# A 2,080-byte pitch for the tiles that TensorE streams in a two-layer hybrid encoder trunk

## Chip, cores and metric

The kernel runs on 1 core of one Trainium2 chip. The metric is the device time of one execution in microseconds. The kernel before takes 2495.84 us (median of 3 runs, 2495.49 to 2499.09).

## What is computed

Two layers over x, 512 tokens of 1,024 channels in float32. Cut to what matters here:

```python
for l in range(DEPTH):
    x = x + 0.5 * swiglu(rms_norm(x, norm_ffn1[l]), ffn1_wi[l], ffn1_wo[l])   # 1024 -> 2 x 2816 -> 1024
    p = rms_norm(x, norm_mix[l]) @ w_in[l]
    x = x + concat(rwkv7(p_a), chunk_attention(p_q, p_k, p_v), pool(p_c)) @ w_out[l]
    x = x + memory_cross_attention(rms_norm(x, norm_cross[l]), rms_norm(mem, norm_mem[l]), ...)
    x = x + 0.5 * swiglu(rms_norm(x, norm_ffn2[l]), ffn2_wi[l], ffn2_wo[l])
```

The four SwiGLU half steps hold most of the arithmetic; then come the input and output projections of the mixers and the four projections of the cross attention.

## The kernel before, in words

Channels lie on the 128 partitions and tokens in the free dimension, so x is eight tiles of 128x512 float32, 2,048 bytes in each partition. Every dense product is made in three passes over exact parts: an operand is split into a high part (a rounded copy by ScalarE, `act` at L75) and a low part (the rest, by VectorE, L69 or L72), and `mm3` issues high x high, high x low and low x high into one PSUM bank (all matmuls of helpers have line L78).

The parts live in three pools. **wp** holds two raw weight tiles of 4,096 bytes (L115, filled by SP's DMA at L116), and three buffers each of `whi` and `wlo` (L149 and L150), 2,048 bytes. A weight tile of 1,024 columns becomes two pairs of `whi` and `wlo`; each holds four slices of 128 columns, 512 bytes apart, that TensorE loads as stationary operand. **hp** holds the eight x tiles and sixteen slots of `hslot` (L83): the normed activations `hhi` and `hlo` for the eight channel blocks k, later the mixers' outputs (`mahi`, `mbhi`, `mchi` and their low parts) and half of the cross attention's (`xohi`, `xolo`). **hid** is opened by each SwiGLU half step and holds 44 tiles `fhi` and `flo` for the 22 blocks of gated values (L282 and L283).

In `ffn`, for each of 22 blocks f, `proj` streams the sixteen h tiles past the weights of the gate (`pg`) and of the up product (`pu`): 8 blocks k times 3 passes, each with its own weight slice. Then ScalarE and VectorE make the gated values and split them. Eight products `po` follow, each streaming the 44 tiles of hid past 22 slices. The mixers (`pin`, `pbvf`, `pout`) stream tiles of hp in the same way, beside the recurrence and the attention, in an order that rates written into the kernel set. In `proj_tok_steps` (`pqk`, `pxq`) the roles are exchanged: 128 tokens of an h tile are stationary and 256 columns of `whi` or `wlo` stream. The cross attention has its own pool with further streamed tiles (`xphi`, `xo`) that the change doesn't touch.

Where a tile lies in its partition follows from the pools, which stand one behind the other in the order in which they are opened: const, wp, hp, tp, bp, and then hid or the pool of a mixer or of the cross attention. In wp and hp all tiles are multiples of 2,048 bytes, so every `whi`, `wlo` and h tile begins at the same place within 2,048 bytes (96 bytes past a multiple). Between hp and hid the one tile that isn't a multiple of 2,048 bytes is `rtok`, 16 bytes that take 32; so the tiles of hid begin 32 bytes further within 2,048 (128 bytes past a multiple).

Of the kernel before, what the change touches and what calls it, by code (L numbers as in the profile page):

```python
# [9 lines left out]
F32R = mybir.dt.float32r  # L10
# [4 lines left out]
P = 128  # L15
T = 512
# [15 lines left out]
LEAD, DENSE_RATE, ATT_RATE = 15, (1.0, 0.61, 0.98), 0.65  # L32
TURN_RATE = (0.5, 0.9)

PAR = {}
# [18 lines left out]
def trunk(tc, I, out, depth=DEPTH):  # L54
    nc = tc.nc
    ctx = ExitStack()
    with ctx:
        const = ctx.enter_context(tc.tile_pool(name="const", bufs=1))
        wp = ctx.enter_context(tc.tile_pool(name="wp", bufs=1))
        hp = ctx.enter_context(tc.tile_pool(name="hp", bufs=1))  # L60
# [21 lines left out]

        def hslot(name, dt=F32R, shape=None):  # L83
            return hp.tile(shape or [P, T], dt, tag="h", name=name, bufs=16)

# [24 lines left out]
        x = [xslot("x") for _ in range(KD)]  # L110
# [20 lines left out]
        ones = const.tile([P, P], F32, name="ones")  # L131
# [6 lines left out]

# [1 line left out]
        def split(o_hi, o_lo, src):  # L140
# [3 lines left out]
        def weights(ap, n):  # L144
            raw = ahead.pop(0) if ahead else load_raw(ap, n)
            r = []
            for c in range(0, n, 512):
                e = min(512, n - c)
                hi = wp.tile([P, 512], F32R, tag="whi", name="whi", bufs=3)  # L149
                lo = wp.tile([P, 512], F32R, tag="wlo", name="wlo", bufs=3)  # L150
                split(hi[:, :e], lo[:, :e], raw[:, c:c + e])
                r.append((hi, lo))
            return r
# [20 lines left out]
        def proj_tok_steps(banks, ap, acts):  # L174
            """banks[i][128 tokens, 2, 256] = act[tokens]^T W, for W = ap [128, 8, 256]."""
            w = []
            for k0 in (0, 4):
                w += weights(ap[:, k0:k0 + 4].rearrange("p k m -> p (k m)"), 1024)
                for k in range(k0, k0 + 4):
                    s = slice(k % 2 * 256, k % 2 * 256 + 256)  # L180
                    wh, wl = w[k // 2]
                    ah, al = acts[k]
                    for b, p in enumerate(banks):
                        for i in range(2):
                            c = slice((2 * b + i) * P, (2 * b + i + 1) * P)
                            st = k == 0 and i == 0
                            mm(p[:, i], ah[:, c], wh[:, s], st, False)
                            mm(p[:, i], al[:, c], wh[:, s], False, False)
                            mm(p[:, i], ah[:, c], wl[:, s], False, k == 7 and i == 1)
                    yield  # L190
# [8 lines left out]

# [1 line left out]
        ssq = {}  # L201
# [13 lines left out]
        def update(k, p, scale=None, spill=False, fetch=None):  # L215
            """x += scale * p; x leaves for DRAM or is fetched from there around the mixers."""
            if fetch is not None:
                x[k] = fetch
                nc.sync.dma_start(out=x[k], in_=x_dram[k])
            if scale is None:  # L220
                tt(x[k], x[k], p, add)
            else:
                stt(x[k], p, scale, x[k], mult, add)
            if spill:
                nc.sync.dma_start(out=x_dram[k], in_=x[k])
            square_in(k)

        def tok_rstd(sq, n, o, scale, e, tag="sm"):
            """o[128 tokens, n / 128] = 1/sqrt(scale * sum over channels of sq + e)."""
            p = bank(tag, "ptok")  # L230
            for i in range(n // P):
                mm(p[:, i:i + 1], sq[:, i * P:(i + 1) * P], ones[:, 0:1])
            act(o, p[:, :n // P], AF.Sqrt, bias=e, scale=scale)
            nc.vector.reciprocal(out=o, in_=o)

        def rstd(bcast=True, tag="sm"):
            """1/rms of x for each token, with the tokens on the rows and, on request, on the columns."""
            rt = tp.tile([P, 4], F32, tag="rtok", name="rtok", bufs=1)
            tok_rstd(ssq["a"], T, rt, 1.0, eps, tag)
            r = None  # L240
            if bcast:
                p = bank(tag, "psn")
                for i in range(4):
                    mm(p[:, i * P:(i + 1) * P], rt[:, i:i + 1].to_broadcast([P, P]), ident)
                r = tp.tile([P, T], F32, tag="rstd", name="rstd", bufs=1)
                act(r, p, AF.Copy)
            return r, rt
# [11 lines left out]

# [1 line left out]
        def ffn(l, which):  # L261
            h = norm(l, f"norm_{which}")
            wi, wo = I[f"{which}_wi"][l], I[f"{which}_wo"][l]
            hid = []
            with tc.tile_pool(name="hid", bufs=1) as hidp:
                for f in range(KF):
# [14 lines left out]
                    tt(u, u, z, mult)  # L281
                    hi = hidp.tile([P, T], F32R, name=f"fhi{f}")  # L282
                    lo = hidp.tile([P, T], F32R, name=f"flo{f}")  # L283
                    split(hi, lo, u)
                    hid.append((hi, lo))
                for m in range(KD):
                    p = bank(ROT[(m + 4) % 8], "po")
# [4 lines left out]

# [1 line left out]
        def mixer(l):  # L294
# [4 lines left out]
            with mx as mp:  # L299
# [29 lines left out]

                # values  # L330
                v = [shifted(6 + j, f"v{j}") for j in range(3)]
# [27 lines left out]

                # the low-rank inputs  # L360
                t9 = shifted(9, "t9")
# [4 lines left out]

                # while x is in DRAM its eight slots hold scratch of the preparation and then q and k of the attention
                # (later its output) and the biases
                xs = [xslot(f"xs{i}") for i in range(8)]
# [63 lines left out]

                # RWKV-7 by chunks of 64, two at a time
                halves = (slice(0, 64), slice(64, 128))
# [19 lines left out]
                def systems(q, o):  # L455
                    """For the pairs 2q and 2q + 1 of chunks, in two sets of heads g, g + 2, g + 4: the masked
                    scores and the inverse of each chunk's triangular system."""
                    nn = mp.tile([P, 2, 3, 2, HD], F32, tag="nn", name="nn", bufs=1)
                    ata, at = [], []
                    for c4 in range(4):  # L460
# [13 lines left out]
                        yield  # L474
                    # doubling the blocks of b: sources in the even blocks, targets in the odd ones. F holds no more
                    # than its blocks, so that the products need a mask only for which blocks pair up; and until
                    # the last step its 32-blocks hold all of it
                    F = []
# [32 lines left out]
                def keyrows(p):  # L511
                    """Keys on the rows, decayed to the chunk's end."""
                    tr = [None, None]
# [16 lines left out]
                def chain(p):  # L530
                    """The state through chunks 2p and 2p + 1, and what they put out."""
                    ata, at, F, tr = sys[p]["ata"], sys[p]["at"], sys[p]["F"], trs[p]
                    y = mp.tile([P, 6, HD], F32, tag="y", name="y", bufs=2)
                    for c2 in range(2):
# [40 lines left out]
                        yield  # L575
                    # group norm, bonus, gate
                    gs = mp.tile([P, 6], F32, tag="gs", name="gs", bufs=2)
# [77 lines left out]

                # attention over all earlier chunks and the own one
                def attend(j, bq, bk, bvt):
# [38 lines left out]
                def pool():  # L696
                    # trailing windows: sums by doubling
                    pwt = mp.tile([P, 2, P], F32, tag="pwt", name="pwt")
                    nc.sync.dma_start(out=pwt, in_=I["poolw"][l])
                    for j in range(2):  # L700
                        def trail(o, i, n):
                            """o = i + i from n tokens before."""
                            nc.gpsimd.tensor_copy(out=o[:, :n], in_=i[:, :n])
                            tt(o[:, n:], i[:, n:], i[:, :T - n], add)
# [55 lines left out]

                # the recurrence sets the pace; the dense products and the attention take steps at these rates beside it
                live = {"r": recurrence(), "d": dense(), "a": attention()}
# [29 lines left out]

# [1 line left out]
        def cross(l):  # L794
            with tc.tile_pool(name=f"cx{l}", bufs=1) as cp:
# [26 lines left out]
                def head(w, acts, n, r, gain, tag, o, b):  # L822
                    """An RMS-normed head; the step it leaves behind puts the channels on the partitions, as high and low parts."""
                    nt = n // P
# [156 lines left out]

# [1 line left out]
def _pack(w, n=P):  # L983
    """[K, M] -> [M / n, 128, K / 128, n]: one contiguous run a partition for each tile of M."""
    K, M = w.shape
    return np.ascontiguousarray(w.reshape(K // P, P, M // n, n).transpose(2, 1, 0, 3))
# [85 lines left out]
```

## Time and profile before

| | |
|---|---|
| median of 3 runs | 2495.84 us (2495.49 to 2499.09) |
| profiled execution, first to last instruction | 2493.6 us; its time as a whole isn't listed |
| TensorE matmul | busy 2460.9 us (99%), 14,058 instructions |
| TensorE weight load | busy 2001.1 us (80%) |
| VectorE, ScalarE, GpSimd | busy 52%, 40%, 7% |
| granted TensorE clock | 1.000 over the span |

Busy matmul time joins intervals that overlap: a matmul's duration is taken from its first column to its end, and the next one starts before that. What a matmul costs TensorE is the distance from its start to the next start, which is shorter than the duration that a row gives; where two groups of matmuls are alike but for their operands and neither waits, their durations differ by what their distances differ. Window counts include an instruction that is cut by the window's edge.

### The profile page before, as it was taken

What the parts mean: (1) busy time and instruction counts of PE and PEld (TensorE: products, weight loads), DVE (VectorE), ACT (ScalarE), POOL (GpSimd) and SP (SyncE); (2) the same over time, 40 slices, a digit from 0 to 9 for tenths busy, and PEclk for the clock granted to TensorE, in tenths of its full rate; (3) what the DMA queues carried; (4) which work ended last, traced back from release to release, by engine and by line L of the source; (5) the groups of instructions that cost most, each with busy time, mean ns of one, the idle gap of its engine ahead of it and who ended that gap; (6) DMA issues with size and microseconds to landing.
All of it is one profiled execution on the core that took longest, in us unless ns stands there. A gap on an engine that the chain in (4) does not pass through costs nothing.

```text
span 2493.6 us, 35631 instructions
## 1 busy us (share of the span) xinstructions
PE 2460.9 (99%) x14058; PEld 2001.1 (80%) x14058; DVE 1300.3 (52%) x2361; ACT 1007.5 (40%) x1804; POOL 184.9 (7%) x246
## 2 busy tenths in 40 slices
PE   8999999999999999999999999999999999999999
PEld 6888887877689888888888888867776898888887
DVE  5444335757575644443344443367676756444422
ACT  4333334434465543333333333343344655433322
POOL 1000002101020000000000000021111201000000
PEclk9999999999999999999999999999999999999999
DMA  3223333210242222323332233322102422222332
GB/s 134 95 99 94 106 114 102 69 45 20 68 143 99 71 93 94 102 93 93 93 99 96 95 98 110 119 72 68 45 25 70 148 88 71 94 100 94 99 110 87
DMA packets 72504, 225.27 MB, mean 90 GB/s; under 512 B 8177, under 2 KB 13201, under 8 KB 72337
## 3 DMA queue, kind: packets, MB, share of 16 engines
q1 hardware_dynamic: 72336, 223.00, 27.5%
q8 instruction: 110, 1.80, 0.3%
q14 instruction: 58, 0.47, 0.1%
HBM read 215.89 MB, written 7.08 MB: 89 GB/s over the span
## 4 chain that ended last, share of the span: by engine, by line
PE 95%; DVE 2%; issue 1%; ACT 1%; DMA 1%; POOL 0%; POOLq 0%; ACTq 0%; DVEq 0%; SPq 0%
PE po L78 20%; PE pu L78 20%; PE pg L78 19%; PE pxq L78 5%; PE pin L78 4%; PE pxw L78 3%; PE pqk L78 3%; PE pout L78 3%; PE pxv L78 2%; PE pbs L78 1%; PE pbvf L78 1%; PE pf L78 1%; PE ptt L78 1%; PE pbo L78 1%; PE pr L78 1%; PE psc L78 1%
## 5 line engine op out<-in xcount | busy, mean ns | idle before, releaser
L75 ACT ACTIVATE whi<-raw 128x512 fp32r<-128x512 f32 (+1 forms) x806 | 493.8, 614 | 964.9 <-PE po L78 323.9
L69 DVE TENSOR_TENSOR wlo<-raw,whi 128x512 fp32r<-128x512 f32 (+1 forms) x806 | 550.5, 685 | 570.4 <-ACT whi L75 566.7
L78 PE MATMUL pg<-hhi,whi 128*128 128x512 f32 x704 | 275.4, 391 | 6.6 <-ACT whi L75 6.6
L78 PE MATMUL po<-fhi,whi 128*128 128x512 f32 x704 | 278.1, 395 | 0.0
L78 PE MATMUL po<-fhi,wlo 128*128 128x512 f32 x704 | 278.1, 395 | 0.0
L78 PE MATMUL po<-flo,whi 128*128 128x512 f32 x704 | 278.1, 395 | 0.0
L78 PE MATMUL pg<-hlo,whi 128*128 128x512 f32 x704 | 275.4, 391 | 2.6 <-DVE hlo L72 2.6
L78 PE MATMUL pu<-hhi,wlo 128*128 128x512 f32 x704 | 274.0, 389 | 0.7 <-DVE wlo L69 0.7
L78 PE MATMUL pg<-hhi,wlo 128*128 128x512 f32 x704 | 274.5, 390 | 0.0
L78 PE MATMUL pu<-hhi,whi 128*128 128x512 f32 x704 | 273.9, 389 | 0.0
L78 PE MATMUL pu<-hlo,whi 128*128 128x512 f32 x704 | 273.9, 389 | 0.0
L69 POOL TENSOR_TENSOR ssa<-ssa,sq 128x512 f32<-128x512 f32 x63 | 86.7, 1377 | 1238.4 <-ACT sq L75 1237.8
L78 PEld LDWEIGHTS pg<-hhi,whi 128*128 128x128 f32 x704 | 132.6, 188 | 34.1 <-ACT whi L75 6.6
L78 PEld LDWEIGHTS po<-flo,whi 128*128 128x128 f32 x704 | 131.9, 187 | 32.4
L78 PEld LDWEIGHTS po<-fhi,whi 128*128 128x128 f32 x704 | 131.9, 187 | 32.4
L78 PEld LDWEIGHTS po<-fhi,wlo 128*128 128x128 f32 x704 | 131.9, 187 | 32.2
L78 PEld LDWEIGHTS pg<-hlo,whi 128*128 128x128 f32 x704 | 132.3, 188 | 31.7 <-DVE hlo L72 4.9
L78 PEld LDWEIGHTS pu<-hhi,wlo 128*128 128x128 f32 x704 | 132.1, 188 | 28.4 <-DVE wlo L69 1.2
L78 PEld LDWEIGHTS pg<-hhi,wlo 128*128 128x128 f32 x704 | 132.6, 188 | 27.6 <-DVE wlo L69 0.3
L78 PEld LDWEIGHTS pu<-hhi,whi 128*128 128x128 f32 x704 | 132.1, 188 | 27.7
L78 PEld LDWEIGHTS pu<-hlo,whi 128*128 128x128 f32 x704 | 132.3, 188 | 27.4
L69 DVE TENSOR_TENSOR z<-pg,rstd 128x512 f32<-128x512 f32 x88 | 60.9, 692 | 134.0 <-PE pg L78 124.4
(305 smaller groups left out, 4010.7 us busy)
## 6 DMA issues: line engine op xcount, KB each, us to landing
raw<-in_ffn_wi_dram SPq DMA_DIRECT2D x175, 512.0 KB, 3.5
raw<-in_ffn_wo_dram SPq DMA_DIRECT2D x64, 512.0 KB, 3.5
raw<-in_w_in_dram SPq DMA_DIRECT2D x30, 512.0 KB, 3.5
raw<-in_ffn_wo_dram SPq DMA_DIRECT2D x32, 384.0 KB, 3.1
raw<-in_x_wk_dram SPq DMA_DIRECT2D x16, 512.0 KB, 3.6
raw<-in_x_wv_dram SPq DMA_DIRECT2D x16, 512.0 KB, 3.5
raw<-in_x_wq_dram SPq DMA_DIRECT2D x16, 512.0 KB, 3.5
raw<-in_w_qk_dram SPq DMA_DIRECT2D x12, 512.0 KB, 3.6
```

The lines of the kernel that those rows point to most:

```text
L69: (eng or nc.vector).tensor_tensor(out=o, in0=a, in1=b, op=op)
L75: nc.scalar.activation(out=o, in_=i, func=f, **k)
L78: nc.tensor.matmul(o, lhsT=w, rhs=x, start=start, stop=stop)
```

## The change

Tiles of `hslot`, of `whi` and `wlo` and of `fhi` and `flo` get rows of 520 elements, of which the first 512 are used. Nothing else in the program is different: the same instructions in the same order with the same shapes. Behind the first longer tile everything in the partition moves up: x by 192 bytes, the pools behind hp by 704 bytes. Comments and docstrings are blanked in the new file (not shown), as are two arguments of `hslot` that no call used.

```diff
+ROW = T + 8
...
-        def hslot(name, dt=F32R, shape=None):
-            return hp.tile(shape or [P, T], dt, tag="h", name=name, bufs=16)
+        def hslot(name, dt=F32R):
+            return hp.tile([P, ROW], dt, tag="h", name=name, bufs=16)[:, :T]
...
-                hi = wp.tile([P, 512], F32R, tag="whi", name="whi", bufs=3)
-                lo = wp.tile([P, 512], F32R, tag="wlo", name="wlo", bufs=3)
+                hi = wp.tile([P, ROW], F32R, tag="whi", name="whi", bufs=3)[:, :T]
+                lo = wp.tile([P, ROW], F32R, tag="wlo", name="wlo", bufs=3)[:, :T]
...
-                    hi = hidp.tile([P, T], F32R, name=f"fhi{f}")
-                    lo = hidp.tile([P, T], F32R, name=f"flo{f}")
+                    hi = hidp.tile([P, ROW], F32R, name=f"fhi{f}")[:, :T]
+                    lo = hidp.tile([P, ROW], F32R, name=f"flo{f}")[:, :T]
```

## Rows read from the trace of the kernel before

**Rows 1.** The page: the span, busy time of each engine, and the chain by engine

```profile
span 2493.6 us, 35631 instructions
...
PE 2460.9 (99%) x14058; PEld 2001.1 (80%) x14058; DVE 1300.3 (52%) x2361; ACT 1007.5 (40%) x1804; POOL 184.9 (7%) x246
...
PE 95%; DVE 2%; issue 1%; ACT 1%; DMA 1%; POOL 0%; POOLq 0%; ACTq 0%; DVEq 0%; SPq 0%
```

**Rows 2.** Stretches: gate and up products, then second products; columns in the first line

```profile
core 0: us, PE busy (x) PEld busy (x) DVE busy (x) ACT busy (x) POOL busy (x), PEclk, DMA share, GB/s
1000.00:1100.00 100.00, 100.00 (x443) 82.84 (x442) 47.05 (x73) 34.74 (x55) 0.00 (x0) 1.00 0.29 95
1140.00:1240.00 100.00, 100.00 (x430) 80.34 (x429) 37.04 (x53) 31.52 (x53) 7.76 (x6) 1.00 0.32 96
```

**Rows 3.** Groups of matmuls by shape: busy us, mean ns | idle before, releaser

```profile
L78 PE MATMUL po<-fhi,whi 128*128 128x512 f32 x704 | 278.1, 395 | 0.0
...
L78 PE MATMUL pg<-hhi,whi 128*128 128x512 f32 x704 | 275.4, 391 | 6.6 <-ACT whi L75 6.6
L78 PE MATMUL pg<-hlo,whi 128*128 128x512 f32 x704 | 275.4, 391 | 2.6 <-DVE hlo L72 2.6
L78 PE MATMUL pg<-hhi,wlo 128*128 128x512 f32 x704 | 274.5, 390 | 0.0
L78 PE MATMUL pu<-hhi,wlo 128*128 128x512 f32 x704 | 274.0, 389 | 0.7 <-DVE wlo L69 0.7
```

**Rows 4.** Timeline of TensorE in the up product and in the second product: start us, duration

```profile
1089.66 0.39 PE L78 MATMUL pu<-hhi,wlo 128*128 128x512 f32 x1
...
1090.34 0.39 PE L78 MATMUL pu<-hhi,wlo 128*128 128x512 f32 x1
...
1189.71 0.40 PE L78 MATMUL po<-fhi,whi 128*128 128x512 f32 x1
...
1190.41 0.39 PE L78 MATMUL po<-fhi,whi 128*128 128x512 f32 x1
```

**Rows 5.** Groups of matmuls by shape: value and output product of the cross attention

```profile
L78 PE MATMUL pxv<-whi,mlo 128*128 128x512 f32 x64 | 25.3, 395 | 0.0
L78 PE MATMUL pxv<-wlo,mhi 128*128 128x512 f32 x64 | 25.3, 395 | 0.0
L78 PE MATMUL pxw<-xohi,whi 128*128 128x512 f32 x64 | 25.3, 395 | 0.0
L78 PE MATMUL pxw<-xolo,whi 128*128 128x512 f32 x64 | 25.2, 393 | 0.0
L78 PE MATMUL pxw<-xohi,wlo 128*128 128x512 f32 x64 | 24.9, 389 | 0.0
```

**Rows 6.** Matmuls of tile pxw, 874 to 880 us: duration ns min/median/max, first and last start

```profile
L78 PE MATMUL pxw<-xo,whi x8: 392/396/402, 876.4 to 878.7; 128*128 128x512 f32 x8
L78 PE MATMUL pxw<-xohi,whi x6: 389/394/397, 873.6 to 879.9; 128*128 128x512 f32 x6
L78 PE MATMUL pxw<-xolo,whi x5: 389/397/398, 873.9 to 879.4; 128*128 128x512 f32 x5
L78 PE MATMUL pxw<-xohi,wlo x5: 387/389/389, 874.1 to 879.7; 128*128 128x512 f32 x5
L78 PE MATMUL pxw<-xo,wlo x4: 396/398/399, 876.9 to 879.0; 128*128 128x512 f32 x4
```

**Rows 7.** Timeline of TensorE in an input projection of the mixer

```profile
390.55 0.39 PE L78 MATMUL pin<-hhi,wlo 128*128 128x512 f32 x1
...
393.95 0.39 PE L78 MATMUL pin<-hhi,wlo 128*128 128x512 f32 x1
```

**Rows 8.** Groups of matmuls by shape: 256 columns of weights stream past tokens

```profile
L78 PE MATMUL pxq<-wlo,hhi 128*128 128x256 f32 x256 | 72.8, 284 | 0.0
...
L78 PE MATMUL pxq<-wlo,mhi 128*128 128x256 f32 x128 | 36.2, 283 | 0.4 <-DVE wlo L69 0.4
```

## The prediction

> **What bounds the kernel now.** I read the page's totals and its chain first: TensorE is busy for 99% of the span and 95% of the chain that ended last is its matmuls; VectorE and ScalarE stand at 52% and 40% [rows 1]. So a time can only come from how fast matmuls follow one another. The windows show that in two stretches of 100 us in which TensorE never pauses and the granted clock is 1.00 (2.4 GHz): 443 matmuls of the gate and up products, but only 430 of the second products, of the same shape [rows 2]. That is 225.7 and 232.6 ns for one (edges counted alike). The timeline gives the same: three up matmuls take 0.68 us, three second products 0.70 us [rows 4]. And the groups by shape: 389 ns duration in pu, 390 and 391 in pg, 395 in po (one of three equal groups of pu and of po stands there), with next to no idle time in front [rows 3]; the difference of 6 ns is the difference in distance again. So **matmuls of one shape, without a wait, differ by 6 ns by which tiles they read.**
>
> What differs is where the tiles lie. In pg and pu the streamed h tile and the weight tile begin at the same place within 2,048 bytes, and the four weight slices at steps of 512; so streamed tile and weight slice agree within 512 bytes always. In po they are 32 bytes apart. Two more groups are apart, and both are slow: the value product of the cross attention streams whi past mlo, 32 bytes apart the other way, 395 ns [rows 5]; and xo, 352 bytes apart, has medians of 396 and 398 ns [rows 6]. The same rows hold the control: xohi and xolo, tiles of hp that agree with the same weights, come right behind xo in the same product and range from 387 to 398, median 389 to 397. So agreement doesn't help at once; after a change of relation some matmuls pass before they run at 389. In the mixer, left alone, h tiles run at that rate too: fifteen starts from 390.55 to 393.95 us, 0.227 us each [rows 7].
>
> **The change part by part.**
>
> *Where tiles lie after it.* Each weight tile is 32 bytes further than the one before (six of them), each h slot too (sixteen), and hp begins 6 x 32 = 192 bytes later. H slot i and weight buffer j are then 192 + 32 x (i - j) bytes apart, taken within 512: they agree for one slot in sixteen. For hid it is 736 + 32 x (i - j): again one in sixteen. The relation also changes with every block k and between high and low part, so nothing stays agreed for long enough to settle.
>
> *Gate and up products.* 4,224 matmuls lose the agreement, except one in sixteen. The price is bounded by 392 (the mean of 395, 393 and 389 over the three groups of xohi and xolo) and 395 (po, pxv) [rows 3, 5]. I take 395, since the relation is wrong nearly always as in po, and not half of the time as in xohi. pu: 2,112 x (395 - 389) = 12.7 us. pg: 2,112 x (395 - 390.7) = 9.1 us. Less a sixteenth: 20.4 us. By the low bound it is 2,112 x 3 + 2,112 x 1.3 = 9 us.
>
> *Mixer projections and output.* pin, pbvf and pout stream h tiles 1,104 times (576, 144 and 384). Their group means hold waits, so what share runs at 389 I can't read from them; from a stretch like rows 7 I take about two thirds: 1,104 x 6 x 2/3 = 4.4 us, between 0 and 6.6.
>
> *Second products.* 2,112 matmuls at 395 are apart now and will be, by other distances. One in sixteen agrees: -0.8 us. Bounds: all of them fall to 389, -12.7 us; or they rise to xo's 397, +4 us.
>
> *Streams of 256 columns* (pqk, pxq). Weights stream past h tiles. With agreement the low weights take 284 ns, and 283 past the memory's tiles, which are 32 bytes off [rows 8]. The 1,344 of them that stream past h tiles change by 1 ns at most: 0, between -1.3 and +1.3 us.
>
> *Everything else.* ScalarE and VectorE write and read the same elements; were they slower by a little, their idle half hides it [rows 1, 2]. SP issues the same DMAs to the raw tiles, whose pitch stays. 704 bytes more are used in a partition, and no buffer is lost. I cost these at nothing.
>
> *Sum.* 20.4 + 4.4 - 0.8 = 24 us. The profiled execution's span of 2,493.6 us, with 2.2 us around it if it was a median run, stands for the median of 2,495.84; so 2,495.8 + 24 = **2,520 us**. With the low price for gate and up and nothing for the mixer it is 2,505; with 395 throughout, and xo's price for po, 2,495.8 + 21.8 + 6.6 + 4 + 1.3 = 2,530. A little above that, 2,536, if a new relation is worse than the three that rows show.
>
> **The rivals.**
>
> *Equal places are the clash (faster).* The agreement in pg and pu could be merely a milder form of a clash that all streams have because each begins where the one before it began. 256 columns more cost 389 - 284 = 105 ns [rows 3, 8], so 512 columns stream in 210 ns; the distance is 227, and up to 17 ns of each matmul are not streaming. If staggering returns half, 8 ns on 7,632 matmuls of 512 columns (4,224 + 2,112 + 1,104 + 192 of xohi and xolo), the time is 2,435; a quarter, 2,465. It decides once pg and pu fall below 389. For it: the 17 ns are real, and thirteen of the sixteen distances stand in no row. Against it: in rows 6 the place of the streamed tile changes twice in six microseconds and no matmul falls under 387. The Trainium skill's TensorE: Matmul & The Clock Gate (Back-to-back issue gap) gives 512 / 2.4 + 2.5 = 216 ns for a single isolated matmul's gap; by that figure a stream rid of all clashes would bring an estimated 11 ns and 2,412 us. No row here shows 216. Chance 0.20.
>
> *Only the second products gain.* They reach 389 and the first ones hold it, because a coarser property of the place counts: 2,495.8 - 12.7 = 2,483. Against it: pxv streams whi from the very place of the h tiles and is slow. Chance 0.06.
>
> *It doesn't matter (same).* Either the 6 ns come from something else than the place, or the relation repeats every 64 bytes: then two of three weight buffers still agree, a third of the first products loses (7.3 + 1.5 us) and two thirds of the second gain (-8.5 us): 2,496 either way. Against the latter: softer evidence, only that xphi and the values, 128 bytes apart, aren't shown to settle. By the Trainium skill's SBUF — State Buffer (Who interferes with whom) TensorE has two independent read ports, one for the streamed operand and one for weights, and never waits on anyone; by that rule the place of a tile is free and the time stays at 2,496. Rows 3 speak against the rule, with 389 against 395 at equal shape and no wait. Chance 0.12.
>
> *The forecast.* Slower, 2,505 to 2,536. Chance 0.62.
>
> **How the numbers follow.** Faster 0.20 + 0.06 = 0.26, same 0.12, slower 0.62. A measurement of this kernel tells about 0.2%, 5 us, from no change. The forecast's own range holds about 0.56; the same case and the small gain add 0.17; to reach 0.8 the range takes in the milder third of the large gain, to 2,455. So 2,455 to 2,536.
>
> **What would show it.** Right: in a stretch of gate and up products the count falls from 443 to about 432 in 100 us, pg and pu stand at 394 to 396 ns, po stays within 2 ns of 395, idle times don't change. The step on po is wrong if po falls to 389. The whole argument is wrong if pg and pu stay at 389 or fall below it; then agreement within 512 bytes is not what made them fast.

## The result and the profile after

The changed kernel takes 2519.12 us (median of four runs, three of them within 2518.60 to 2519.33) against 2497.37 us before in the same set of runs: 1.0085 times, 95% interval 1.0069 to 1.0101. It is slower by 0.7 to 1.0%, about 22 us. One of its four runs in that set took 4946 us with its matmuls stretched (pg at 695 ns), and it was the profiled one, so the profile shown here is that of the same kernel run once more (e1 below).

First the page of the changed kernel: the span, the engines, the chain by engine.

```profile
span 2516.4 us, 35631 instructions
...
PE 2485.5 (99%) x14058; PEld 2004.9 (80%) x14058; DVE 1303.2 (52%) x2361; ACT 1009.0 (40%) x1804; POOL 185.5 (7%) x246
...
PE 95%; DVE 2%; ACT 1%; issue 1%; DMA 0%; POOL 0%; POOLq 0%; ACTq 0%; SPq 0%; DVEq 0%
```

The same number of instructions, 22.8 us more span, and 24.6 us more busy time on TensorE; the shares of the other engines stand where they stood [rows 1]. So no wait has appeared: TensorE does the same list of matmuls more slowly.

Some 3 to 5 us of the 22.8 are the granted clock and not the change. Over the span it is 0.998 in this trace and 1.000 in that of the kernel before. It was lower in three stretches of 25 us (columns as in [rows 2]; the kernel before has 1.00 in the stretches that correspond); in the last 25 us it was 0.97, but no matmul became slower there:

```profile
0.00:25.00 25.00, 15.87 (x43) 10.21 (x44) 16.54 (x17) 14.02 (x23) 10.90 (x11) 0.93 0.53 186
1675.00:1700.00 25.00, 24.60 (x106) 17.59 (x106) 17.52 (x29) 11.63 (x17) 4.38 (x7) 0.93 0.19 64
1975.00:2000.00 25.00, 22.83 (x174) 21.87 (x174) 15.45 (x33) 13.80 (x37) 0.00 (x0) 0.93 0.44 148
```

The times agree: beside e1, the kernel before took 2495.2 and 2495.3 us at a mean clock of 1.000 and 2498.3 to 2500.8 at 0.998, and the changed kernel 2518.5 to 2519.4 at 0.998. At an equal clock the change costs some 20 us.

The windows, a stretch of gate and up products and one of second products, say which matmuls became slower:

```profile
core 0: us, PE busy (x) PEld busy (x) DVE busy (x) ACT busy (x) POOL busy (x), PEclk, DMA share, GB/s
1000.00:1100.00 100.00, 100.00 (x432) 80.78 (x431) 46.83 (x73) 34.19 (x54) 0.00 (x0) 1.00 0.29 95
1150.00:1250.00 100.00, 100.00 (x433) 81.04 (x432) 38.63 (x54) 32.16 (x54) 7.76 (x6) 1.00 0.32 97
```

443 matmuls in 100 us have become 432 in the first stretch; the second had 430 and now has 433 [rows 2]. Busy and clock are the same 100% and 1.00 in both. The groups by shape, with the mean duration in ns behind the comma:

```profile
L79 PE MATMUL pg<-hhi,whi 128*128 128x512 f32 x704 | 279.1, 396 | 6.4 <-ACT whi L76 6.4
L79 PE MATMUL pg<-hhi,wlo 128*128 128x512 f32 x704 | 279.0, 396 | 0.0
L79 PE MATMUL pg<-hlo,whi 128*128 128x512 f32 x704 | 278.8, 396 | 2.0 <-DVE hlo L73 2.0
L79 PE MATMUL pu<-hhi,wlo 128*128 128x512 f32 x704 | 278.5, 396 | 0.7 <-DVE wlo L70 0.7
L79 PE MATMUL po<-fhi,whi 128*128 128x512 f32 x704 | 277.7, 394 | 0.0
L79 PE MATMUL pu<-hhi,whi 128*128 128x512 f32 x704 | 277.6, 394 | 0.0
L79 PE MATMUL pu<-hlo,whi 128*128 128x512 f32 x704 | 277.1, 394 | 0.0
L79 PE MATMUL po<-flo,whi 128*128 128x512 f32 x704 | 276.9, 393 | 0.0
L79 PE MATMUL po<-fhi,wlo 128*128 128x512 f32 x704 | 276.7, 393 | 0.0
```

pg and pu went from 389 to 391 up to 394 to 396, po from 395 down to 393 or 394, and the idle time in front of each group is what it was to a few tenths [rows 3]. Within one window of 100 us one can see that this isn't a mean over good and bad stretches (matmuls of pu, min/median/max):

```profile
L79 PE MATMUL pu<-hlo,whi x72: 387/392/399, 999.8 to 1099.5; 128*128 128x512 f32 x72
L79 PE MATMUL pu<-hhi,wlo x72: 390/396/404, 1000.0 to 1099.7; 128*128 128x512 f32 x72
L79 PE MATMUL pu<-hhi,whi x72: 388/396/399, 1000.2 to 1099.9; 128*128 128x512 f32 x72
```

The same three groups of the kernel before, in the same window:

```profile
L78 PE MATMUL pu<-hlo,whi x76: 389/389/389, 999.7 to 1099.6; 128*128 128x512 f32 x76
L78 PE MATMUL pu<-hhi,wlo x76: 389/389/389, 999.9 to 1099.9; 128*128 128x512 f32 x76
L78 PE MATMUL pu<-hhi,whi x75: 389/389/389, 1000.1 to 1099.4; 128*128 128x512 f32 x75
```

Before, all 227 take 389 ns to the nanosecond; after, they spread from 387 to 404. What was the same for each matmul before isn't any more.

### The profile page after: what moved, and what is told of

The parts are those of the page before. It is cut to its first block, busy times and chain, and to the rows that moved or that the text cites. A ratio compares the mean times of both kernels' runs of the same rounds, so it can differ in the third digit from the quotient of the medians.

```text
span 4944.1 us, 35631 instructions
## 1 busy us (share of the span) xinstructions
PE 4928.4 (100%) x14058; PEld 3292.0 (67%) x14058; DVE 1311.4 (27%) x2361; ACT 1019.1 (21%) x1804; POOL 178.6 (4%) x246
## 4 chain that ended last, share of the span: by engine, by line
PE 100%; ACT 0%; DMA 0%; POOLq 0%; issue 0%; DVE 0%; SPq 0%; ACTq 0%
PE pu L79 21%; PE pg L79 21%; PE po L79 20%; PE pin L79 6%; PE pxq L79 5%; PE pout L79 4%; PE pxw L79 4%; PE pqk L79 3%; PE pxv L79 2%; PE pbvf L79 1%; PE pbs L79 1%; PE pf L79 1%; PE ptt L79 1%; PE pbo L79 1%; PE pxs L79 1%; PE pxo L79 1%
## 5 line engine op out<-in xcount | busy, mean ns | idle before, releaser
L79 PE MATMUL pg<-hhi,whi 128*128 128x512 f32 x704 | 489.4, 695 | 7.1 <-ACT whi L76 7.1
L79 PE MATMUL pg<-hlo,whi 128*128 128x512 f32 x704 | 489.3, 695 | 0.0
L79 PE MATMUL pg<-hhi,wlo 128*128 128x512 f32 x704 | 487.9, 693 | 0.0
L79 PE MATMUL pu<-hhi,wlo 128*128 128x512 f32 x704 | 487.4, 692 | 0.0
L79 PE MATMUL pu<-hlo,whi 128*128 128x512 f32 x704 | 486.5, 691 | 0.0
L79 PE MATMUL pu<-hhi,whi 128*128 128x512 f32 x704 | 486.5, 691 | 0.0
L79 PE MATMUL po<-fhi,whi 128*128 128x512 f32 x704 | 474.8, 674 | 0.0
L79 PE MATMUL po<-flo,whi 128*128 128x512 f32 x704 | 474.6, 674 | 0.0
L79 PE MATMUL po<-fhi,wlo 128*128 128x512 f32 x704 | 474.5, 674 | 0.0
L79 PEld LDWEIGHTS pg<-hhi,wlo 128*128 128x128 f32 x704 | 215.1, 306 | 124.9 <-issue 117.5
L79 PEld LDWEIGHTS po<-fhi,whi 128*128 128x128 f32 x704 | 208.6, 296 | 120.6 <-issue 112.7
```

The costliest lines, as they stand in the source:

```text
L79: nc.tensor.matmul(o, lhsT=w, rhs=x, start=start, stop=stop)
```

## The experiments

The theory was that of the prediction: a matmul is fast when the tile that streams and the weight slices begin at the same place within some number of bytes (512 as the prediction had it), and the longer pitch destroys this.

**e1: the changed kernel again.** No edit.

> The changed kernel once more, for its profile. Theory (agreement: a matmul of 512 columns takes 389 ns when the streamed tile and the weight slice begin at the same place within 512 bytes, about 395 when they don't): pu and pg at 394 to 396, po at 394 to 396, 430 to 433 matmuls in 100 us of the gate and up products, 2,517 to 2,521 us. Rival (the time went elsewhere, to idle time or to the splits): pu stays at 389 and the idle time in front of the groups grows by some 20 us.

2518.96 us, 1.0080 times the kernel before (1.0066 to 1.0094), and the rows above. Idle time didn't grow, the durations did. The rival falls.

**e2 and e3: half of the change each.** e2 gives only hid the longer pitch, e3 only the h slots and the weight tiles.

```diff
# e2: before.py with
+ROW = T + 8
-                    hi = hidp.tile([P, T], F32R, name=f"fhi{f}")
+                    hi = hidp.tile([P, ROW], F32R, name=f"fhi{f}")[:, :T]
...
# e3: before.py with
+ROW = T + 8
-            return hp.tile(shape or [P, T], dt, tag="h", name=name, bufs=16)
+            return hp.tile([P, ROW], dt, tag="h", name=name, bufs=16)[:, :T]
-                hi = wp.tile([P, 512], F32R, tag="whi", name="whi", bufs=3)
+                hi = wp.tile([P, ROW], F32R, tag="whi", name="whi", bufs=3)[:, :T]
...
```

> Only the tiles of hid get the longer pitch; h and weight tiles stay at 2,048. Agreement: pu and pg stay at 389, po was apart from its weights and is apart still for fifteen tiles in sixteen, so 394 to 396 and 2,493 to 2,499 us. Rival (a longer pitch costs by itself, wherever it is): po rises by about as much as pu did in the changed kernel, 2,112 x 6 ns, to 2,508 us.

> Only the h slots and the weight tiles get the longer pitch; hid stays at 2,048. Agreement: all of the loss is here, pu and pg at 394 to 396, 2,515 to 2,522 us. Rival (the pitch costs by itself in each place): less than the changed kernel by the part of hid, 2,508 us.

e2: 2498.80 us, 0.9997 times before (0.9988 to 1.0006). e3: 2518.56 us, 1.0078 (1.0064 to 1.0092). So all of the loss is in the h and weight tiles, and a longer pitch costs nothing by itself in hid, whose products were slow already: in e2 po stands at 394 and 395 and pu at 390 (389 before; e2's granted clock in its first 25 us is 0.93).

**e4: the opposite of the change.** If agreement is what makes a matmul fast, the slow groups can be given it. The small tiles that shift hid and the cross attention's pool are padded to 512 bytes each; all else stays at 2,048.

```diff
-            rt = tp.tile([P, 4], F32, tag="rtok", name="rtok", bufs=1)
+            rt = tp.tile([P, P], F32, tag="rtok", name="rtok", bufs=1)[:, :4]
...
-                rmt = cp.tile([P, 2], F32, tag="rmt", name="rmt")
+                rmt = cp.tile([P, P], F32, tag="rmt", name="rmt")[:, :2]
...
-                        st = cp.tile([P, 6], F32, tag="xst", name="xst", bufs=4)
+                        st = cp.tile([P, P], F32, tag="xst", name="xst", bufs=4)[:, :6]
```

(The tiles xqg and xqs likewise.)

> Pitch 2,048 everywhere, and small tiles of tp and of the cross attention's pool are given 512 bytes each, so that hid, the memory's parts, the values, xphi and xo all begin where the weight slices do within 512 bytes. Agreement: po falls from 395 to 389 (2,112 x 6 ns = 12.7 us), pxv, pxo and xo too (480 x 6 ns = 2.9 us): 2,479 to 2,484 us. Rival (gate and up products are fast for another reason than the place, as their tiles being in hp): po stays at 395 and the time at 2,496.

2483.86 us, 0.9941 times before (0.9927 to 0.9955): faster than both kernels. Groups by shape of e4:

```profile
L78 PE MATMUL pu<-hhi,wlo 128*128 128x512 f32 x704 | 274.6, 390 | 0.7 <-DVE wlo L69 0.7
...
L78 PE MATMUL po<-fhi,whi 128*128 128x512 f32 x704 | 273.9, 389 | 0.0
L78 PE MATMUL po<-flo,whi 128*128 128x512 f32 x704 | 273.9, 389 | 0.0
L78 PE MATMUL po<-fhi,wlo 128*128 128x512 f32 x704 | 273.9, 389 | 0.0
...
L78 PE MATMUL pxv<-whi,mlo 128*128 128x512 f32 x64 | 25.0, 391 | 0.0
...
L78 PE MATMUL pxv<-wlo,mhi 128*128 128x512 f32 x64 | 24.9, 390 | 0.0
```

and the second products' window:

```profile
1140.00:1240.00 100.00, 100.00 (x443) 82.84 (x442) 36.77 (x52) 31.27 (x52) 7.73 (x6) 1.00 0.32 98
```

po runs at the 389 ns that only pu had, 443 in 100 us where there were 430 [rows 2], and pxv fell from 395 to 390 and 391 [rows 5]. The medians differ by 15.6 us, as expected; the span of this trace is only 11.6 us shorter, but its mean clock is 0.998 and that of the trace before 1.000.

**e5, e6, e7: which distances are good.** hid is opened anew by each of the four half steps, so a filler of a different length in each gives po four distances from the weight slices in one run.

```diff
+PAD = {(0, 'ffn1'): 480, (0, 'ffn2'): 32, (1, 'ffn1'): 96, (1, 'ffn2'): 224}
...
             with tc.tile_pool(name="hid", bufs=1) as hidp:
+                if PAD[l, which]:
+                    hidp.tile([P, PAD[l, which] // 4], F32, name="pad")
```

> Pitch 2,048 everywhere; a filler in hid puts its tiles 0, 64, 128 and 256 bytes past the place of the weight slices (within 512) in the four SwiGLU half steps, in the order in which they run; it was 32 in all four. Agreement within 512 bytes: po at 389 ns in the first half step alone, 394 to 396 in the other three. Rival (the relation repeats every 64 bytes): 389 in all four. Rival (every 128 or 256): 389 at 0, and at 128 and 256 or at 256 alone. Rival (equal places are a milder clash): one of the three goes below 389.

> As the one before, with 96, 160, 192 and 224 bytes. Agreement within 512 bytes: 394 to 396 in all four. Rival (equal places are a milder clash, and a distance exists that clashes less): one of them below 389.

> As the one before, with 288, 320, 384 and 448 bytes. Agreement within 512 bytes: 394 to 396 in all four. Rival (equal places are a milder clash): one of them below 389.

Each took one run (2491.49, 2499.92 and 2496.11 us, beside 2498.43 before). What counts is in the rows: matmuls of po in 90 us of each half step, min/median/max. e5, distances 0, 64, 128, 256 bytes:

```profile
L79 PE MATMUL po<-fhi,whi x133: 389/389/389, 269.7 to 359.4; 128*128 128x512 f32 x133
...
L79 PE MATMUL po<-flo,whi x132: 388/388/388, 1129.8 to 1219.8; 128*128 128x512 f32 x132
L79 PE MATMUL po<-fhi,wlo x132: 392/392/392, 1130.0 to 1220.0; 128*128 128x512 f32 x132
L79 PE MATMUL po<-fhi,whi x131: 394/394/394, 1130.3 to 1219.5; 128*128 128x512 f32 x131
...
L79 PE MATMUL po<-fhi,whi x129: 392/392/398, 1489.8 to 1579.4; 128*128 128x512 f32 x129
L79 PE MATMUL po<-flo,whi x129: 392/398/398, 1490.0 to 1579.6; 128*128 128x512 f32 x129
...
L79 PE MATMUL po<-flo,whi x133: 389/389/389, 2369.6 to 2459.4; 128*128 128x512 f32 x133
```

At 0 and at 256 po takes 389. At 128 it takes 392 or 398. At 64 it stands between: 388, 392 and 394 for the three passes, 391 in the mean, and no nanosecond of spread in 395 matmuls. So the period is 256, not 512, not 128 and not 64. e6, distances 96, 160, 192:

```profile
L79 PE MATMUL po<-fhi,whi x130: 392/392/392, 269.7 to 360.0; 128*128 128x512 f32 x130
L79 PE MATMUL po<-flo,whi x129: 394/394/394, 269.9 to 359.5; 128*128 128x512 f32 x129
L79 PE MATMUL po<-fhi,wlo x129: 399/399/399, 270.1 to 359.7; 128*128 128x512 f32 x129
...
L79 PE MATMUL po<-flo,whi x129: 392/397/400, 1129.8 to 1219.7; 128*128 128x512 f32 x129
...
L79 PE MATMUL po<-flo,whi x129: 394/394/394, 1489.8 to 1579.4; 128*128 128x512 f32 x129
```

At 224 (not shown) all three passes have medians of 395 or 396. e7 has 288, 320, 384 and 448, which are 32, 64, 128 and 192 past 256; two rows of its second half step, at 320:

```profile
L79 PE MATMUL po<-fhi,wlo x132: 392/392/392, 1129.8 to 1219.7; 128*128 128x512 f32 x132
L79 PE MATMUL po<-fhi,whi x132: 394/394/394, 1130.0 to 1220.0; 128*128 128x512 f32 x132
```

320 repeats 64 to the nanosecond (its third pass is at 388 too), and the other three repeat theirs: medians of 394 to 396 at 288, as at 32 before; 392, 395 and 398 at 384, 395 in the mean as at 128; 394 at 448. Of the eight distances in a period that are multiples of 32 bytes, one is fast, one lies between, six take some 394 to 397 ns. From the first start to the last, the 528 second products of a half step take 119.5 us at 0 and 256, 120.6 at 64 and 320, 123.5 at 160 and 123.0 at the others, so from start to start a bad distance costs 6.7 ns a matmul. None lies below 389 in the mean of its three passes, so for these distances the rival in which equal places are a milder clash falls.

**e8: is it the place or the relation?** The six weight tiles alone are moved by 32 bytes; a second filler behind them keeps everything else where it was within 256.

```diff
         nc.sync.dma_start(out=cst, in_=I["cst"])
+        wp.tile([P, 8], F32, tag="fill", name="fill", bufs=1)
+        last = []
...
+                if not last:
+                    last.append(wp.tile([P, 56], F32, tag="rest", name="rest", bufs=1))
                 split(hi[:, :e], lo[:, :e], raw[:, c:c + e])
```

> Pitch 2,048 everywhere; the six weight tiles alone move up by 32 bytes, everything behind them by 256. So they now begin where the tiles of hid and the memory's parts do, and 32 bytes past the h tiles (all within 256). Agreement of the streamed tile with the weight slice: the groups change places, po 395 to 389, pxv to 390, pu and pg 389 to 395; 2,112 x 6 and 192 x 6 ns gained, 4,224 x 5.5 ns and some 4 us in the mixers lost: 2,506 to 2,514 us. Rival (the place of the streamed tile itself, whatever it meets): h tiles and hid lie within 256 bytes where they lay before, so nothing changes, 2,497 us.

2512.56 us, 1.0050 times before (1.0034 to 1.0065). The groups changed places, though within 256 bytes neither the h tiles nor hid had moved:

```profile
L78 PE MATMUL pg<-hhi,wlo 128*128 128x512 f32 x704 | 279.5, 397 | 0.0
L78 PE MATMUL pu<-hhi,wlo 128*128 128x512 f32 x704 | 278.9, 396 | 0.7 <-DVE wlo L69 0.7
...
L78 PE MATMUL po<-fhi,whi 128*128 128x512 f32 x704 | 273.9, 389 | 0.0
...
L78 PE MATMUL pxv<-whi,mlo 128*128 128x512 f32 x64 | 25.0, 391 | 0.0
```

It is the relation: po and pu load their slices from the same weight tiles and went opposite ways, so it isn't the place of the weights alone, and within 256 bytes the streamed tiles had not moved.

**e9: another pitch that keeps the relation.** e3 with rows of 2,304 bytes.

```diff
-ROW = T + 8
+ROW = T + 64
```

> h slots and weight tiles at a pitch of 2,304 bytes, hid at 2,048. Agreement within 256 bytes: all h and weight tiles still agree, pu 389 to 390, pg 390 to 392, the time of before (2,494 to 2,502 us). Rival (any pitch off the 2,048 costs, or the agreement counts within 512, where half of the pairs now differ): pu and pg between 392 and 396, 2,505 to 2,520 us.

2498.72 us, 0.9997 times before (0.9989 to 1.0006). Three groups of e9:

```profile
L79 PE MATMUL po<-fhi,whi 128*128 128x512 f32 x704 | 278.1, 395 | 0.0
...
L79 PE MATMUL pg<-hhi,wlo 128*128 128x512 f32 x704 | 274.9, 391 | 0.0
L79 PE MATMUL pu<-hhi,wlo 128*128 128x512 f32 x704 | 274.7, 390 | 0.7 <-DVE wlo L70 0.7
```

This pitch isn't a power of two, but a multiple of 256; it costs nothing and brings nothing (here too the clock of the first 25 us is 0.93, which is in the groups' means). Half of the pairs differ by 256 within 512 here, so this shows the period once more, in other groups.

## Why the prediction was right

It said 2,520 us and slower; 2519.12 was measured. The mechanism holds: what TensorE streams and what it loads lost their common place, and the gate and up products pay for it. That the number was met to 1 us is luck. The 24 us were added to a median near that of runs at a clock of 1.000, while the changed kernel ran at 0.998; at an equal clock the change costs 18 us by the traces (below) and 20 by the times. The sum was 4 to 6 us too high, and the clock made up for it. Below, times by starts run from one matmul's start to another's, in stretches whose clock is 1.00.

- **What bounds the kernel.** TensorE's rate alone, right: no new wait, the shares of the other engines unchanged.
- **Gate and up products.** Predicted 20.4 us at 395 ns. By busy times of the groups pg grew by 836.9 less 825.3 and pu by 833.2 less 821.8, together 23.0 us; but the first half step lies partly in a stretch at 0.93. The second half step, the kernel before and then the changed one (min/median/max, first and last start):

```profile
L78 PE MATMUL pg<-hhi,whi x176: 389/389/486, 882.0 to 1117.1; 128*128 128x512 f32 x176
L78 PE MATMUL po<-fhi,whi x176: 393/396/399, 1123.2 to 1245.7; 128*128 128x512 f32 x176
L79 PE MATMUL pg<-hhi,whi x176: 388/396/475, 888.3 to 1129.2; 128*128 128x512 f32 x176
L79 PE MATMUL po<-fhi,whi x176: 388/396/400, 1135.5 to 1257.2; 128*128 128x512 f32 x176
```

  From the first pg to the first po it is 241.2 us before and 247.2 after. The three later half steps grew by 5.94, 4.83 and 5.26 us; four times their mean is 21.4 us. The size is right to 1 us, though a matmul that loses its place loses 6.7 ns by starts and not 6, and agreement is more frequent than one in sixteen (next point).
- **How often tiles still agree.** The step that was wrong in kind: "the same place within 512 bytes", one in sixteen. The runs show 256, so one in eight agrees, and one in eight more, at 64, lies between at 391. The mean over the eight distances of e5 to e7 and of before, 389, 395, 391, 395, 395, 396, 394 and 395.5, is 394, near what pu and po come to when the distances are mixed: 394 to 396 and 393 to 394. That a mixture always costs the mean isn't shown. In e3 each half step's second products meet the six weight tiles at 224, 192, 160, 128, 96 and 64 bytes, never at 0, and still the 528 take 122.0 to 122.1 us by starts, where they took 123.0 before.
- **Second products.** Predicted -0.8 us. Busy times 831.3 less 834.3, -3.0 us; by starts 123.0 us a half step became 122.0 to 122.2, together -3.5. More of the new distances are good than one in sixteen; e3 says that this isn't all of it, and the rest stays open.
- **Mixers, output product and streams of 256 columns.** Predicted 4.4 us, and 0 within 1.3 us. By busy times pin grew by 3.1, pout by 0.9, pbvf by 0.4, the xohi and xolo groups by 0.5; the streams of 256 columns past h tiles fell by 2.0; pxq past the memory's tiles grew by 1.6. Most of pin's growth, and all of that of pxq past the memory's tiles, is the clock of the stretches at 1675 and 1975 us. In the first layer, without such a stretch, those pxq groups are the same before and after (18.4, 18.2 and 18.1 us), and e2, which moves neither them nor the weights, has its first one at 37.4 us too, with 0.93 at 1950 to 1975. From the last po of the first half step to the first pg of the second, all of the first layer's mixers and cross attention, it is 504.2 us before and 504.2 after. So this term was oversized: about 1 us is lost there and as much comes back. By starts a matmul of pin, pbvf and pout lost some 1.7 ns there and not the 4 of the sum; why isn't shown.
- **The sum.** 21.4 - 3.5 + 0 is 18 us by starts at full clock, 24 predicted. The other 5 us of the 22.8 between the two spans are the three stretches at 0.93.
- **The rivals.** A large gain from staggering: none of the distances tried is better than 0. A gain of the second products while the first hold their rate isn't what the change does, but it can be had: e4 is 0.59% faster than before (0.45 to 0.73%), some 15 us, beside the 12.7 that the prediction gave po alone and 2.9 expected of the cross attention's groups. No effect because the relation repeats every 64 bytes: falls with e5. (Its price was off as well: with steps of 32 bytes about half of the pairs would still agree, in both products, not two thirds; that makes some 2,503 us and not 2,496.) No effect because the place of a tile is free, as the prediction worked it out from the rule of the Trainium skill's SBUF — State Buffer (Who interferes with whom): falls with e4 and e8, in which nothing but places differs and po moves from 395 to 389; the measurement decides.

What stays open is why. The traces show that the relation of the streamed tile to the weight slices counts, that 256 bytes is the period, and that the cost is 6.7 ns on 226.7. Which of the two slices counts, the one in the array or the one that is loaded beside the stream, wasn't tried: at a pitch of 2,048 or 2,304 both have the same place within 256, and the mixture at 2,080, where they differ, wasn't taken apart.

## What to carry to other kernels

Where matmuls follow one another without a wait and groups of one shape still differ in duration, compare where their operands begin: here equal places within 256 bytes were worth 6.7 ns in 233 for each matmul, and padding a handful of small tiles brought 0.6% of the kernel. The pitch chosen to stagger the tiles undid an agreement that nobody had planned; before a layout is changed, the fast group is to be found and its property kept. Before the parts of a difference are added up from two traces, their granted clocks are to be compared stretch by stretch: here 3 to 5 of 22.8 us were the clock. A layout experiment can be had four at a time when a pool is opened anew for each stage.

## What the runs showed of the hardware that was not expected

A stream of matmuls finds a pattern and keeps it. At distance 0 each took 389 ns, without an exception in the 90 us window; at 64 the passes took 388, 392, 394 over and over, at 96 392, 394, 399, at 192 always 394. Durations alone mislead here: the sums of three at 96 and 192, 1185 and 1182, differ, but by starts both distances take 123.0 us for 528 matmuls. After a change of partner some matmuls pass until the pattern stands [rows 6].

With a pitch of 2,080 the distance changes at almost every matmul, and the durations spread; but that isn't disorder. In e3's second products between 1140 and 1240 us, 98% of the durations are those of 66 matmuls before (one product of 22 slices in three passes), and in the changed kernel's gate and up products between 900 and 1120 us 89% are those of 72 before (three products, after which the same weight buffers come round). The pattern has become long.

At equal places the settled matmul is not the shortest: at 64 one pass in three is at 388, and in the changed kernel single ones reach 387. The mean of the mixture is worse all the same.
